# Places for the first rows of y, and the engine for the low parts of the output weights, in a hybrid gMLP and SSD layer on one core

## The chip, the cores and the metric

The kernel runs on one core of a Trainium2 chip. The metric is the device time of one execution in microseconds (us): the median of several runs. The profile comes from one more execution, whose own time is given beside its span.

Engines are named as in the profile: PE (TensorE, matmuls), DVE (VectorE), ACT (ScalarE), POOL (GpSimd), SP (SyncE, which here issues nearly all loads). Each takes its instructions in one fixed order and waits at the head of it.

## The reference, cut

One layer over 1024 positions of width 1024: a gMLP branch (y_a), a Mamba-2 SSD branch (y_b, 2048 wide, 8 groups), a gated merge, an output projection and a last normalisation. All inputs are float32.

```python
proj = h @ w_in
y_a = spatial_gating(gelu(gm_u), gelu(gm_v), ...) * silu(gm_z)
y_b = ssd_scan(xh, dt, a, bm, cm) + xh * d_skip[:, None]
yz = (y_b.reshape(b, s, 2048) * silu(ssm_z)).reshape(b, s, 8, 256)
y_b = rms_norm(yz, ssm_norm_w.reshape(8, -1)).reshape(b, s, 2048)
merged = sigmoid(g_a) * (y_a @ w_proj_a) + sigmoid(g_b) * (y_b @ w_proj_b)
x = x + gate[:, None, :] * (merged @ w_out)
return rms_norm(x, final_norm_w)
```

## The kernel before, in words

Large products run in fp32r with three matmuls for one: each operand is split into a high part (ACT casts it to fp32r) and a low part (the difference, cast again), and high by high, high by low and low by high are summed in PSUM. Besides, y_b @ w_proj_b and merged @ w_out are computed block by block with seven products instead of eight (Strassen's scheme): p1 to p7 for the first, seven of PRODUCTS for the second.

The kernel's last 300 us run through three stages that matter here.

**SSD.** `step` takes the 8 groups and their chunks one after the other. `front` makes the product sp of the states, `back` the product yn of the state before, and `evacuate` takes yn out of PSUM: DVE multiplies (ym, L1262), POOL adds and multiplies by the gate (L1264, L1265); the result is stored to DRAM (yb_d). Sums of squares over a group follow on POOL (L1293; L1285 for the last two groups), then matmuls with ones (pq) and a short chain that gives the factor of the RMS norm, rs_d in DRAM. Between these, `proj_a` fills PE with the matmuls of y_a @ w_proj_a (pma); `wa_load` loads its raw weights into a ring of four places, war_r.

**p1 to p7** (from L1636 on). `loads(u)` issues, six units ahead, on SP: for a unit with fresh rows `y_load` (first rb, the factor of a group, for even n; then yn, 128 rows of y), then the weights. `operands(u)`, four units ahead, normalises these rows (`y_norm`, DVE, in place) and splits them into `{p}bh`, `{p}bl`. The places of 128x512 come from a list, room, in which places are put in the order in which they come free, and from which each load takes the first. Three rings are cut from room: rb_r (factors), bh_r and bl_r (high and low parts). The order on each engine is that of a scheduler that follows the program with priorities and its own estimates; so a place decides what a load waits for, and can also move instructions.

**The output product.** `gate_load` and `merged` make the left operands: `split` gives a11, s1, s2, a22, s4, a12 their high and low parts, with s4 from `fourth` (L1786). `wo_load` loads a block of w_out, `wo_split` (L1795) makes its high part on ACT and its low part in place on DVE (L1798). A name such as wlt13 is the block t1 of quarter 3, `wlb110` the block b11 of quarter 0, wlt21 the block t2 of quarter 1. The places of high parts are reused under the name of the first that had them (ma11h, mwhb).

Of the kernel before, what the change touches and what calls it, by code (L numbers as in the profile page):

```python
# [35 lines left out]
def hybrid_kernel(  # L36
# [7 lines left out]
    V, A, G, PE = nc.vector, nc.scalar, nc.gpsimd, nc.tensor  # L44
# [42 lines left out]
    def f32(t):  # L87
        return t.bitcast(F32)
# [1284 lines left out]
    room = [f"{nm}{v}{k}" for nm in BN for v in "hl" for k in range(4)]  # L1373
# [4 lines left out]
    def ring(n):  # L1378

        return [room.pop(0) for _ in range(n)], [0]  # L1380
# [20 lines left out]
    war_r, wah_r, wal_r = [], [], []  # L1401
# [130 lines left out]
    tha_r, ea_r, y1_r, ym_r = (ring(c) for c in (4, 3, 2, 2))  # L1532
# [86 lines left out]
    def slot_tile(name, dt=F32):  # L1619
        tag = room.pop(0)  # L1620
        t = hp.tile([P, 512], dt, name=name, tag=tag)
        tags_of[name] = tag
        return t
# [12 lines left out]

    first, rest = room[:3], room[10:21]
    del room[10:21], room[:3]
    rb_r, bh_r, bl_r = (([first[n]] + [rest.pop(0) for _ in range(c)], [0]) for n, c in enumerate((3, 4, 4)))
    yt, rbs = {}, {}  # L1640

    def y_load(n, h):
# [89 lines left out]
    def place(name):  # L1732
        if not places and m_sl:
            pool, b = m_sl.pop(0)
            t = pool.tile([P, 3, 512], F32R, name=f"m{name}", tag="sl", bufs=b)
            places.extend(t[:, i] for i in range(3))
        return (places.pop(0), None) if places else (slot_tile(name, F32R), name)
# [57 lines left out]
    def wo_split(nm, j):  # L1795
        hi, t = place(f"wh{nm}{j}"), wor.pop((nm, j))
        A.copy(hi[0], f32(t))
        V.tensor_sub(t, f32(t), f32(hi[0]))  # L1798
        opb[nm, j] = [hi, (t, f"wl{nm}{j}")]

    rows = {}
# [21 lines left out]
            groups[7].post2(1, groups[7].late[:1])  # L1823
    draw(left[0] + 1)
    room.extend(tag for k in (KT - 2, KT - 1) for tag in ya_tags[k])
    for tags, _ in (war_r[0], wah_r[0], wal_r[0], tha_r):
        room.extend(tags)
    ps1.__exit__(None, None, None)
    ps3 = tc.tile_pool(name="ps3", bufs=1, space=PSUM, reuse_waits="tile")
# [3 lines left out]

    BESIDE = [(j // 2, wo_load, ("b11", j)) for j in range(4)] + [(2 + j, wo_load, ("t1", j)) for j in range(4)]
    BESIDE += [(2 + j, wo_split, ("b11", j)) for j in range(4)]
    BESIDE += [(3 + j, row_load, (j,)) for j in range(5)] + [(j + 4, split, ("s1", j - 1)) for j in (1, 3)]
    for u, (nm, k) in enumerate(units):
        if k == 0:
            if nm == "p1":
                first = {t: psb.tile([P, 512], F32, name=f"{t}p", tag=f"b{t}") for t in ('x0', 'x1', 'x2', 'x3', 'y3', 'y1', 'y2', 'y0')}  # L1840
# [25 lines left out]
        if k == KT - 1:  # L1866
            for j in range(4):
                with tc.high_priority():
                    if nm in ("p1", "p3", "p5"):
                        t = slot_tile(f"{nm}_{j}")  # L1870
# [83 lines left out]
    for nm, bn, pn, first, t0, c, done in PRODUCTS:  # L1954
# [4 lines left out]
        def beside(j):  # L1959
            if nm == "s1":  # L1960
                fourth(j)
            for b in LOADS.get(nm, ()):
                wo_load(b, j)
            if nm == "a11" and j < 3:
                row_load(5 + j)
            if (na, j) in raw:
                last["split"] = split(na, j).ins
            for b in SPLITS.get(nm, ()):
                wo_split(b, j)
# [34 lines left out]
    lo, hi = slice(0, 256), slice(256, 512)  # L2004
# [63 lines left out]
```

## Time and profile before

| | |
|---|---|
| median of 3 runs | 1365.38 us (1363.75 to 1366.4) |
| profiled execution | 1363.33 us, span 1361.5 us, granted PE clock 0.997 |
| PE busy | 99% of the span |
| DVE, ACT, POOL busy | 78%, 59%, 14% |
| L1264, L1265 (POOL, 128x512) | 1281 ns and 1386 ns in the mean |
| L1798 (DVE, 128x512) | 671 to 687 ns |
| L1652, normalisation of y (DVE) | 763 ns in the mean, 32 of them |

In the stages named above, by the clock of the span: SSD ends with the last pq matmuls at about 1122 us, p1 begins at 1123.59, the output product follows p4, whose last matmuls run about 1276, and the last stores end the span.

A row of a timeline reads: start in us, duration in us, engine, line, operation, output <- inputs with their shapes, and in brackets how long the engine stood idle before it and what released it.

### The profile page before, as it was taken

What the parts mean: (1) busy time and instruction counts of PE and PEld (TensorE: products, weight loads), DVE (VectorE), ACT (ScalarE), POOL (GpSimd) and SP (SyncE); (2) the same over time, 40 slices, a digit from 0 to 9 for tenths busy, and PEclk for the clock granted to TensorE, in tenths of its full rate; (3) what the DMA queues carried; (4) which work ended last, traced back from release to release, by engine and by line L of the source; (5) the groups of instructions that cost most, each with busy time, mean ns of one, the idle gap of its engine ahead of it and who ended that gap; (6) DMA issues with size and microseconds to landing.
All of it is one profiled execution on the core that took longest, in us unless ns stands there. A gap on an engine that the chain in (4) does not pass through costs nothing.

```text
span 1361.5 us, 20111 instructions
## 1 busy us (share of the span) xinstructions
PE 1347.4 (99%) x6907; PEld 1114.0 (82%) x6907; DVE 1055.5 (78%) x1731; ACT 801.4 (59%) x1446; POOL 195.4 (14%) x193
## 2 busy tenths in 40 slices
PE   8999999999999999999999999999999999999997
PEld 6688888888888888888888888888888888788886
DVE  5777786787777898687887788458888866959976
ACT  5754666666656665456576655486877743333443
POOL 1000000000000000000000000007898971000002
PEclk9999999999999999999999999999999999999999
DMA  9675444433345667777656865489889858978913
GB/s 294 174 249 151 123 124 124 118 123 117 108 125 155 193 190 228 243 233 237 199 194 189 248 203 184 159 289 312 306 293 313 306 207 313 332 260 314 381 45 124
DMA packets 249577, 288.64 MB, mean 212 GB/s; under 512 B 16860, under 2 KB 196484, under 8 KB 249476
## 3 DMA queue, kind: packets, MB, share of 16 engines
q1 hardware_dynamic: 174868, 203.80, 47.0%
q10 hardware_dynamic: 74544, 83.57, 18.0%
q8 instruction: 54, 0.88, 0.3%
q14 instruction: 47, 0.39, 0.1%
q0 software_dynamic: 64, 0.00, 0.0%
HBM read 199.82 MB, written 87.49 MB: 211 GB/s over the span
## 4 chain that ended last, share of the span: by engine, by line
PE 86%; DMA 8%; DVE 3%; SPq 1%; issue 1%; ACT 0%; POOL 0%; POOLq 0%; DVEq 0%; ACTq 0%
PE xcb L585 6%; PE xz L585 6%; PE xuz L585 6%; PE xx L585 6%; PE pma L82 6%; PE xg L585 6%; PE yuz L585 3%; PE yx L585 3%; PE ycb L585 3%; PE yz L585 3%; PE vx L990 3%; PE yg L585 3%; PE ox L1909 3%; PE yi L82 2%; PE sp L82 2%; PE oy L1909 2%
## 5 line engine op out<-in xcount | busy, mean ns | idle before, releaser
L1159 POOL TENSOR_SCALAR_AFFINE_SELECT dcy<-dcy 128x1024 f32<-128x1024 f32 x32 | 35.3, 1102 | 789.1 <-DMA yl<-ya_d 745.8
L1167 ACT ACTIVATE dcy<-dcy,nacs 128x128 f32<-128x128 f32 x256 | 78.3, 389 | 2.8 <-POOL dcy L1159 2.3
L1183 DVE TENSOR_TENSOR dcy<-dcy,pc 128x1024 f32<-128x1024 f32 x32 | 39.0, 1219 | 7.8 <-PE pc L85 5.7
L1265 POOL TENSOR_TENSOR yz<-y,sl 128x512 f32<-128x512 f32 x32 | 44.4, 1386 | 2.5
L82 PE MATMUL pma<-yh,wah 128*128 128x512 f32 x128 | 43.2, 418 | 0.0
L82 PE MATMUL pma<-yh,wal 128*128 128x512 f32 x128 | 42.6, 413 | 0.0
L82 PE MATMUL pma<-yl,wah 128*128 128x512 f32 x128 | 40.2, 395 | 0.0
L1155 ACT ACTIVATE ea<-dcy 64x512 f32<-64x512 f32 x64 | 39.8, 622 | 0.4
L1190 ACT COPY bn<-pc 128x256 f32<-128x256 f32 x32 | 11.9, 371 | 46.8 <-DVE dcy L1183 45.9
L1652 DVE SCALAR_TENSOR_TENSOR yn<-yn,par,rb 128x512 f32<-128x512 f32 x32 | 24.4, 763 | 17.9 <-DMA yn<-yb_d 16.2
L1060 ACT ACTIVATE ac<-ac 128x1024 f32<-128x1024 f32 x32 | 33.9, 1061 | 7.4 <-DVE ac L1058 7.3
L1058 DVE SCALAR_TENSOR_TENSOR ac<-c2x,cwt,ac 128x1023 f32<-128x1023 f32 (+2 forms) x24 | 30.7, 1280 | 8.7 <-ACT ac L1056 8.6
L1264 POOL TENSOR_TENSOR y<-y,ym 128x512 f32<-128x512 f32 (+1 forms) x32 | 37.0, 1155 | 2.1 <-DVE ym L1262 2.1
L1058 DVE SCALAR_TENSOR_TENSOR ac<-c2cb,cwt,ac 128x1023 f32<-128x1023 f32 (+2 forms) x24 | 30.7, 1279 | 8.1 <-ACT ac L1056 8.0
L1924 POOL TENSOR_TENSOR r<-r,fnw 128x512 f32<-128x512 f32 x4 | 6.1, 1533 | 205.3 <-ACT junk L1922 205.3
L82 PE MATMUL yi<-dcy,xd 128*64 128x128 f32 x512 | 35.0, 279 | 0.0
L1262 DVE TENSOR_TENSOR ym<-yn,ea 128x512 f32<-128x512 f32 (+1 forms) x32 | 19.9, 621 | 18.2 <-PE yn L82 18.1
L82 PE MATMUL sp<-xe,bn 128*128 128x256 f32 x112 | 32.7, 409 | 0.0
L82 PEld LDWEIGHTS yn<-sl,st 128*128 128x128 f32 x224 | 29.7, 191 | 2.8 <-POOL st L1228 0.4
L82 PEld LDWEIGHTS yi<-dcy,xd 128*64 128x64 f32 x512 | 27.3, 136 | 5.7 <-issue 2.9
L1058 DVE SCALAR_TENSOR_TENSOR ac<-c1cb,cwt,ac 128x1023 f32<-128x1023 f32 (+2 forms) x24 | 30.6, 1276 | 1.3 <-ACT ac L1056 1.3
L1022 ACT ACTIVATE vm<-vm,vr 128x128 f32<-128x128 f32 x64 | 25.6, 483 | 9.6 <-DMA vm<-v_d 9.1
(2983 smaller groups left out, 4369.7 us busy)
## 6 DMA issues: line engine op xcount, KB each, us to landing
sl<-s_d SPq DMA_DIRECT2D x32, 768.0 KB, 6.9
s_d<-ac ACTq DMA_DIRECT2D x32, 512.0 KB, 3.3
wb_d<-wbb ACTq DMA_DIRECT2D x32, 512.0 KB, 3.8
dcy<-acs_d SPq DMA_DIRECT2D x32, 512.0 KB, 4.6
av<-in_w_in_dram SPq DMA_DIRECT2D x36, 256.0 KB, 3.5
aw<-in_ada_w_dram SPq DMA_DIRECT2D x16, 512.0 KB, 6.1
wbr<-in_w_proj_b_dram SPq DMA_DIRECT2D x32, 256.0 KB, 4.5
yb_d<-yz ACTq DMA_DIRECT2D x32, 256.0 KB, 6.0
```

The costliest lines, as they stand in the source:

```text
L82: pin(PE.matmul(acc, l, r, start=first, stop=last))
L585: pin(PE.matmul(ps, lw[:, k * P : (k + 1) * P], r[k], start=first and n + k == 0, stop=n == 2 and k == 3, skip_group_check=not first))
L990: pin(PE.matmul(ps[pn][j], l[:, j * P : (j + 1) * P], r, start=nm in ("p1", "p5", "p2") and n + units[i][1] == 0, stop=n == 2 and k == 3, ...
L1058: V.scalar_tensor_tensor(ac[:, s:], cc[:, : S - s], conv_wt[:, 3 - s, i : i + 1], ac[:, s:], op0=ALU.mult, op1=ALU.add)
L1060: A.activation(ac, ac, AF.Silu)
L1155: link("A", lambda: A.activation(ea[hh * HD : (hh + 1) * HD], dcy.rearrange("p (j e) i l -> p e j (i l)", e=2)[hh * HD : (hh + 1) * HD, hh ...
L1159: link("G", lambda: G.affine_select(out=d8, in_=d8, compare_op=ALU.is_ge, fill=-1e30, base=0, pattern=[[0, 2 * HPG], [1, P]], channel_mult ...
L1167: link("A", lambda: A.activation(dcy[:, h, i, :], dcy[:, h, i, :], AF.Exp, bias=sub[:, i, h : h + 1]))
L1183: link("V", lambda: V.tensor_tensor(d3, d3, pc[:, 0:256].unsqueeze(1).to_broadcast([P, HPG, 256]), op=ALU.mult))
L1264: link("G", lambda: G.tensor_add(y1[:, :, t0:], y1[:, :, t0:], m[:, :, t0:]))
L1265: link("G", lambda: G.tensor_mul(yz, y1, sl[:, 4:6]))
L1909: pin(PE.matmul(ps, a[:, tsl], b[:, cs], start=first and n + j == 0, stop=n == 2 and j == 3, skip_group_check=not first))
```

## The change

Two things are changed.

The rings of p1 to p7 are cut anew. Before, each of rb_r, bh_r and bl_r got one of the three places first (which have held ea, the decays of the SSD stage) and the others from rest; now rb_r gets all three and one of rest, bh_r and bl_r five of rest each. And the four places of `wa_load` (war_r) are put at the front of room at once, instead of at its end after the last product of the first projection; so the first four loads of y (yn0 to yn3) take them. Before, yn0 took the place of the SSD state (st) and yn1 to yn3 places of y_a.

The low parts in `wo_split` are made by POOL instead of DVE: 28 operations of 128x512.

```diff
     first, rest = room[:3], room[10:21]
     del room[10:21], room[:3]
-    rb_r, bh_r, bl_r = (([first[n]] + [rest.pop(0) for _ in range(c)], [0]) for n, c in enumerate((3, 4, 4)))
+    rb_r, bh_r, bl_r = ((first[:n] + [rest.pop(0) for _ in range(c)], [0]) for n, c in ((3, 1), (0, 5), (0, 5)))
+    room[:0] = war_r[0][0]
...
     def wo_split(nm, j):
         hi, t = place(f"wh{nm}{j}"), wor.pop((nm, j))
         A.copy(hi[0], f32(t))
-        V.tensor_sub(t, f32(t), f32(hi[0]))
+        G.tensor_sub(t, f32(t), f32(hi[0]))
         opb[nm, j] = [hi, (t, f"wl{nm}{j}")]
...
     room.extend(tag for k in (KT - 2, KT - 1) for tag in ya_tags[k])
-    for tags, _ in (war_r[0], wah_r[0], wal_r[0], tha_r):
+    for tags, _ in (wah_r[0], wal_r[0], tha_r):
         room.extend(tags)
```

Lines behind L1639 count one more after the change.

SP keeps its order; only what its loads wait for changes. These are its rows at the first loads of y (behind each in brackets the engines whose counters it waits for; rb0 and yn0, yn1 are as in the text above, p1r the raw weights of p1):

```order
-L91 DMA yn0_0_10925<-yb_d0_91 128x512 [waits DMAHW3_49,DVE_49,PE_49]
-L91 DMA p1r0_10928<-in_w_proj_b_dram 128x512 [waits DMAHW5_49]
-L91 DMA yn1_0_10930<-yb_d1_92 128x512 [waits DMAHW0_49,PE_49]
-L91 DMA p1r1_10933<-in_w_proj_b_dram 128x512 [waits DMAHW2_49,Activation_49]
-L91 DMA rb2_0_10935<-rs_d1_59 128x512 [waits DMAHW4_49,PE_49]
-L91 DMA yn2_0_10937<-yb_d2_93 128x512 [waits DMAHW6_49]
+L91 DMA yn0_0_10925<-yb_d0_91 128x512 [waits DMAHW0_49]
+L91 DMA p1r0_10928<-in_w_proj_b_dram 128x512 [waits DMAHW2_49,DVE_49,PE_49]
+L91 DMA yn1_0_10930<-yb_d1_92 128x512 [waits DMAHW3_49]
+L91 DMA p1r1_10933<-in_w_proj_b_dram 128x512 [waits DMAHW4_49,DVE_49,Activation_49]
+L91 DMA rb2_0_10935<-rs_d1_59 128x512 [waits DMAHW5_49]
+L91 DMA yn2_0_10937<-yb_d2_93 128x512 [waits DMAHW7_49]
```

yn0 no longer waits for PE or DVE; p1r0, which now stands first in line with a wait for engines, waits for PE's product sp7_2 and p1r1 for DVE's ym6_3. (Before, yn0 waited for PE's last product yn7_3, and all that follows behind it.)

On DVE the normalisations of y have moved up. This is the end of the SSD stage after the change, from the evacuation of group 7's chunk pair 2 on; before, the rows of L1653 (then L1652) stood behind those of L1305:

```order
 L1236 TENSOR_TENSOR st22_8261<-st22_8261,sp7_2_10712 128x256
+L1653 SCALAR_TENSOR_TENSOR yn0_0_10925<-yn0_0_10925,par2_147,rb0_0_10923 128x512
 L1262 TENSOR_TENSOR ym7_2_10749<-yn7_2_10743,ea7_2_10375 128x512
 L1183 TENSOR_TENSOR dcy7_3_10526<-dcy7_3_10526,pc7_3_10754 128x1024
```

```order
+L1653 SCALAR_TENSOR_TENSOR yn1_0_10930<-yn1_0_10930,par2_147,rb0_0_10923 128x512
 L1262 TENSOR_TENSOR ym6_3_10804<-yn6_3_10799,ea6_3_10456 128x512
 L1236 TENSOR_TENSOR st_8258<-st_8258,sp7_3_10819 128x256
 L1216 SCALAR_TENSOR_TENSOR y17_3_10822<-sl7_3_10528,dskt_151,yi7_3_10810 128x256 x2
+L1653 SCALAR_TENSOR_TENSOR yn2_0_10937<-yn2_0_10937,par2_147,rb2_0_10935 128x512
 L1262 TENSOR_TENSOR ym7_3_10841<-yn7_3_10836,ea7_3_10530 128x512
```

Each of yn0, yn1 and yn2 is now normalised ahead of one of the last three evacuations, which wait for it in order.

On ACT, in the output product, the high part of a12 for quarter 2 has moved ahead of two high parts of weights. Before:

```order
L1797 CAST ma11h1_12273<-wlt12_12316 128x512
L1755 CAST ma11h1_12273<-s1_3_12190 128x512
L1797 CAST wht22_12558<-wlt22_12463 128x512
L1797 CAST mwhb112_12318<-wlt13_12345 128x512
L1755 CAST mwhb112_12318<-p1_0_11222 128x512
L1755 CAST a12h2_12904<-tg6_0_12341 128x512
```

After:

```order
L1798 CAST ma11h1_12273<-wlt12_12316 128x512
L1756 CAST ma11h1_12273<-s1_3_12190 128x512
L1756 CAST a12h2_12904<-tg6_0_12341 128x512
L1798 CAST wht22_12558<-wlt22_12463 128x512
L1798 CAST mwhb112_12318<-wlt13_12345 128x512
L1756 CAST mwhb112_12318<-p1_0_11222 128x512
```

a12h2 waits for DVE's s4_2 (`s4_2_12550`, L1786, now L1787). In the same stretch POOL, which had nothing to do there, now makes these low parts in this order:

```order
+L1799 TENSOR_TENSOR wlb110_12214<-wlb110_12214,ma11h0_12220 128x512
+L1799 TENSOR_TENSOR wlb111_12216<-wlb111_12216,ma11h1_12273 128x512
+L1799 TENSOR_TENSOR wlb112_12247<-wlb112_12247,mwhb112_12318 128x512
+L1799 TENSOR_TENSOR wlb113_12249<-wlb113_12249,mwhb113_12347 128x512
+L1799 TENSOR_TENSOR wlt10_12267<-wlt10_12267,ma11h0_12220 128x512
+L1799 TENSOR_TENSOR wlt21_12443<-wlt21_12443,wht21_12534 128x512
+L1799 TENSOR_TENSOR wlt11_12298<-wlt11_12298,ma11h1_12273 128x512
+L1799 TENSOR_TENSOR wlt12_12316<-wlt12_12316,ma11h1_12273 128x512
+L1799 TENSOR_TENSOR wlt22_12463<-wlt22_12463,wht22_12558 128x512
+L1799 TENSOR_TENSOR wlt13_12345<-wlt13_12345,mwhb112_12318 128x512
```

wlt13's low part is the tenth; 18 more follow. On DVE the same 28 rows are gone, and three operations stand ahead of p4bl7 that stood behind it.

## The prediction

> **What bounds the kernel now.** I read the page's shares first, then the chain that ended last, then busy time by stage, then what TensorE (PE) waits for.
>
> ```profile
> PE 1347.4 (99%) x6907; PEld 1114.0 (82%) x6907; DVE 1055.5 (78%) x1731; ACT 801.4 (59%) x1446; POOL 195.4 (14%) x193
> PE 86%; DMA 8%; DVE 3%; SPq 1%; issue 1%; ACT 0%; POOL 0%; POOLq 0%; DVEq 0%; ACTq 0%
> ```
>
> TensorE is busy 99% of the span and fills 86% of the chain. Work that other engines shed therefore gains only where TensorE is shown idle. The same view by stage (columns: stretch, length, busy time of PE, PEld, DVE, ACT, POOL) shows what stands close behind it:
>
> ```profile
> 1100.00:1150.00 50.00, 50.00 (x280) 40.46 (x279) 33.39 (x54) 17.30 (x32) 21.00 (x17) 1.00 0.71 244
> 1150.00:1200.00 50.00, 49.40 (x216) 39.97 (x215) 41.49 (x67) 13.85 (x24) 0.00 (x0) 1.00 0.92 331
> 1250.00:1300.00 50.00, 49.40 (x219) 40.56 (x217) 50.00 (x84) 22.56 (x40) 0.00 (x0) 1.00 0.97 366
> ```
>
> From 1250 to 1300 us VectorE (DVE) has no idle time, and there the new GpSimd work falls. TensorE's waits that the change can touch are two, each with its row in the timeline:
>
> ```profile
> PE oy L1909 <- DVE wlt L1798: 0.6, 1, 0.6
> PE x0p L1717 <- DVE p6bl L1691: 0.5, 1, 0.5
> 1290.02 0.39 PE L1909 MATMUL oy<-ma11h,s1l 128*128 128x512 f32 x1
> 1290.24 0.39 PE L1909 MATMUL oy<-mwhb,ma11h 128*128 128x512 f32 x1
> 1291.23 0.50 PE L1909 MATMUL oy<-wlt,ma11h 128*128 128x512 f32 x1 [0.60 <-DVE wlt L1798]
> 1167.13 0.39 PE L1717 MATMUL x0p<-p6bh,p6a 128*128 128x512 f32 x1
> 1168.06 0.50 PE L1717 MATMUL x0p<-p6bl,p6a 128*128 128x512 f32 x1 [0.55 <-DVE p6bl L1691]
> ```
>
> Matmuls otherwise start 0.22 to 0.23 us apart (1290.02 to 1290.24), so the first place loses about 0.9 us with its slow restart and the second 0.7, some 1.3 with smaller ones behind it. **All that the change can win is 2.2 us**, 0.16% of 1363.
>
> **Part A, the first rows of y.** Four loads of y go to places that are free; their places before were held until the last state product.
>
> ```profile
> 1095.90 0.37 SPq L91 DMA_DIRECT2D rb<-rs_d  x1
> 1110.42 0.32 SPq L91 DMA_DIRECT2D yn<-yb_d  x1
> 1112.82 0.32 SPq L91 DMA_DIRECT2D yn<-yb_d  x1
> ...
> DMA to landing us min/median/max: 4.4/5.5/6.5
> ```
>
> The first load now goes right behind rb, at about 1096.3 instead of 1110.42, and lands 4.4 to 6.5 us later (the last row gives all 24 loads of y): 1100.7 to 1102.8. SP runs in order, so p1r0 and p1r1, which inherit the waits, still hold what stands behind them; the second y goes when the product sp7_2 is done, the third after the evacuation ym6_3. Nothing in p1 (from 1123.59 on) waited for y, so early arrival is worth nothing there.
>
> But the normalisations of these rows have moved up in VectorE's order, and VectorE too runs in order: yn0's stands ahead of the evacuation ym7_2. Behind that evacuation hangs GpSimd's (POOL's) last chain:
>
> ```profile
> 1100.08 0.69 DVE L1262 TENSOR_TENSOR ym<-yn,ea 128x512 f32<-128x512 f32 x1 [1.55 <-PE yn L82]
> 1100.85 1.28 POOL L1264 TENSOR_TENSOR y<-y,ym 128x512 f32<-128x512 f32 x1 [0.60 <-DVE ym L1262]
> 1109.49 1.27 POOL L1293 TENSOR_TENSOR yz<-yz 128x512 f32<-128x512 f32 x1
> 1111.24 0.65 PE L82 MATMUL pq<-yz,ones 128*32 128x128 f32 x16
> 1118.13 1.46 POOL L1285 TENSOR_TENSOR lq<-lq,lq 128x512 f32<-128x512 f32 x1 [3.02 <-ACT lq L1281]
> 1121.73 0.43 PE L82 MATMUL pq<-lq,ones 128*32 128x128 f32 x8
> ```
>
> Step by step: yn0 lands at 1100.7, its normalisation takes 0.75 (row of 1117.69 below), so ym7_2 starts at about 1101.5, 1.4 late. From 1100.85 POOL works almost without a gap until 1110.76, the end of the sum of squares that the second half of these 16 pq matmuls reads. That half starts at about 1111.5, so the chain has 0.75 of slack. A second normalisation (yn1) falls beside the chain and holds one of its operations for 0.67, the cadence of such an operation. 1.4 + 0.67 − 0.75 = **+1.3 us** in which TensorE, in order, stands at pq. Bounds: 0, if yn0 lands before 1100.1 (some other transfer of this trace would have to be its model, none of the 24 is), 2.4 if it lands at the median and 3.4 at the slowest; I keep 0 to 3.4. The third normalisation delays ym7_3, but pq7_1, which hangs on it, comes only at 1121.73, 2.1 us after its sum ends (1118.13 + 1.46), and hides it.
>
> **Part B, p6.** Its stall hangs on rows that SP loads late:
>
> ```profile
> SPq L91 <- DMA rs_d<-ssq: 3.7, 1, 3.7
> ```
>
> That wait is for the factor of the last groups, not for a place. The re-cut rings leave it as it is: 0, with −1.3 as the other end.
>
> **Part C, the low parts on GpSimd.** Twenty-eight operations leave VectorE and enter POOL. On VectorE one starts 0.60 us after another. On POOL the same shape takes 1.27 to 1.29 where VectorE leaves it alone. What decides is whether the two run beside each other:
>
> ```profile
> 1113.82 1.29 POOL L1285 TENSOR_TENSOR lq<-lq,lq 128x512 f32<-128x512 f32 x1
> 1114.37 1.28 DVE L1652 SCALAR_TENSOR_TENSOR yn<-yn,par,rb 128x512 f32<-128x512 f32 x1 [1.66 <-issue]
> 1117.69 0.75 DVE L1652 SCALAR_TENSOR_TENSOR yn<-yn,par,rb 128x512 f32<-128x512 f32 x1 [2.03 <-DMA yn<-yb_d]
> 1340.52 3.51 DVE L1932 SCALAR_TENSOR_TENSOR r<-r,dde,fnw 128x1024 f32<-128x1024 f32 x2
> 1341.49 1.45 POOL L1924 TENSOR_TENSOR r<-r,fnw 128x512 f32<-128x512 f32 x1 [3.03 <-ACT junk L1922]
> 1345.15 1.27 DVE L1932 SCALAR_TENSOR_TENSOR r<-r,dde,fnw 128x1024 f32<-128x1024 f32 x1
> 1345.52 2.06 POOL L1924 TENSOR_TENSOR r<-r,fnw 128x512 f32<-128x512 f32 x1 [2.58 <-ACT junk L1922]
> 1102.16 0.68 DVE L1186 TENSOR_TENSOR xd<-px,dthq 128x512 f32<-128x512 f32 x1
> 1102.21 1.29 POOL L1265 TENSOR_TENSOR yz<-y,sl 128x512 f32<-128x512 f32 x1
> ```
>
> They do not. A normalisation beside POOL's sum takes 1.28, alone 0.75; two L1932 beside one POOL operation take 3.51, where the single one of 1345.15 takes 1.27, so one POOL operation's length is added. POOL's operation of 2.06 us waited in turn for that single one. With two operands in SBUF on both sides they take turns, one and one, even with VectorE's next operation queued. The last pair shows the exception: a VectorE operation that reads PSUM (px) runs beside POOL undisturbed.
>
> [...]
>
> So VectorE is not relieved: each low part that falls beside it costs it POOL's 1.25 instead of its own 0.60. The path to the matmul of 1291.23:
>
> ```profile
> 1285.09 0.67 DVE L1786 TENSOR_TENSOR s<-tg,p 128x512 f32<-128x512 f32 x1
> 1285.76 0.62 ACT L1797 CAST mwhb<-wlt 128x512 fp32r<-128x512 f32 x1
> 1286.80 0.62 ACT L1755 CAST a12h<-tg 128x512 fp32r<-128x512 f32 x1
> 1290.51 0.67 DVE L1798 TENSOR_TENSOR wlt<-wlt,mwhb 128x512 fp32r<-128x512 f32 x1
> ```
>
> Before, ACT made wlt13's high part at 1285.76, ahead of a12h2, and VectorE its low part at 1290.51. Now a12h2 stands ahead of the high parts of wlt22 and wlt13 in ACT's order, and it waits for VectorE's s4_2, the row of 1285.09.
> - Ahead of s4_2, eight low parts run on POOL (wlb110 to wlb113, wlt10, wlt21, wlt11, wlt12) while VectorE is full: 8 × 1.25, less 0.6 that falls beside an operation that reads PSUM: +9.4. Five low parts have left VectorE there: −3.0. One other operation now stands behind s4_2: −0.6. So s4_2 ends at 1285.7 + 5.8 = 1291.5.
> - Then ACT's a12h2, wht22 and wlt13's high part at 0.52 each: 1293.1.
> - POOL first makes wlt22's low part, from about 1292.5 with a turn of VectorE before it, to 1294.2, lets one VectorE operation through (0.6), and ends wlt13's low part at 1296.1. TensorE reads it at 1291.23 now: **+4.9 us**.
>
> Some 1.5 to 2 us of this appear already at the last step of p4:
>
> ```profile
> 1271.26 0.67 DVE L1691 TENSOR_TENSOR p4bl<-yn,p4bh 128x512 fp32r<-128x512 f32 x1
> 1274.83 0.39 PE L1717 MATMUL x0p<-p4bl,p4a 128*128 128x512 f32 x1
> ```
>
> VectorE's p4bl7 is ready 2.9 before its matmul; four low parts at 0.65 more and three operations put ahead of it at 0.60 make it 4.4 late. That is part of the 4.9, since a TensorE held here arrives later there. What comes after has this room:
>
> ```profile
> 1300.00:1362.00 62.00, 54.71 (x253) 45.62 (x251) 43.07 (x79) 26.12 (x61) 9.01 (x9) 0.97 0.17 68
> ```
>
> The remaining 18 low parts cost VectorE 0.65 each, but from 1300 on it has 19 us of idle time (43.07 busy of 62); I add 0.3. **C = +5.2.** Bounds: if VectorE were not held at all, POOL's six low parts from wlt10 to wlt13, begun at about 1282.7 at 1.27 each, end at 1290.3 and the stall goes: −0.9. If each low part took 2.06 (the longest POOL row of the shape) instead of 1.27, the eight on the path add 8 × 0.8 = 6.4: +11.6.
>
> **The sum.** A +1.3, B 0, C +5.2: +6.5 us. The profiled execution took 1363.33 us (span 1361.5), so 1369.8; the median of the three runs, 1365.38, lies 2.05 above the profiled one, so the median becomes 1371.9, say **1372.0**.
>
> **Rivals.**
> 1. *VectorE is truly relieved* (the other side): POOL's writes rounded to fp32r, in place, do not take turns with VectorE, or the turns fall into gaps. Then C is −0.9, and with y early p6 may gain up to 1.3; part A hidden. Time 1365.4 − 0.9 to − 2.2: 1363.2 to 1364.5, within 0.2%. It decides by one point: whether s4_2 ends before about 1286. For it: nothing between 1250 and 1300 uses POOL today (0.00), so no row shows this mixture. Against it: every pair of such operands above, without exception, took turns.
> 2. *The low part is dear on POOL*: 2.06 us each, or POOL is served only after several VectorE operations, since none of the rows has a VectorE queue that is full for 50 us. C up to +11.6: 1378.3. Against it: the undisturbed rows are all at 1.27 to 1.29, and the row of 3.51 shows POOL served at once.
> 3. *Part A does nothing*: y lands in time or the pq slack is larger; only C counts. 1370.6. For it: the slack is read from one group of 16 matmuls whose halves the row doesn't part. Against: none of 24 loads landed under 4.4 us.
> 4. *The weights' part is not on the path*: a12h2 does not hold ACT, because s4_2 is early enough. Then wlt13's low part is the last of six in POOL from 1283.3 on, each of 1.27 with a turn of 0.6 after it: about 1294.5 against 1291.23: C +3.3, A +1.3, 1370.0.
>
> **How the numbers follow.** The sum 0.58 (with its own spread of 1368 to 1376), rival 1 0.13, rival 2 0.11, rival 3 0.10, rival 4 0.08. The range 1366.5 to 1378.5 leaves out rival 1 and the upper part of rival 2. A measurement of this kernel can tell about 0.2%, 2.7 us, from no change. Faster by more would need more than the 2.2 us that TensorE idles at these places: 0.03. Within 0.2%: rival 1 and the low edge of the other cases: 0.17. Slower: 0.80.
>
> **What would show it.** A: an idle time of about 1.3 us ahead of the pq matmuls near 1111, with ym7_2's row starting after yn0's normalisation near 1101.5. No such gap: A is wrong. C: VectorE rows of 1.8 to 1.9 us between 1262 and 1300 beside POOL rows of L1799, s4_2 ending near 1292 to 1294, TensorE idle by about 2 us at the end of p4 and about 3 more at `oy<-wlt`, now released by POOL. VectorE rows that stay at 0.67 beside POOL rows would refute the turns and with them the forecast. B: the 0.55 at p6 stays.

## The result and the profile after

The changed kernel takes 1369.96 us in the median of 22 runs (1364.68 to 1373.29), the one before 1366.43 us in the same runs: **ratio 1.003, interval 1.002 to 1.0039**, 3.5 us slower by the medians. In a second set of runs (experiment e1) it was 1.0026 (1.0015 to 1.0038). The profiled execution took 1364.68 us, span 1363.0, granted clock 0.999; it is the shortest of the 22.

The page's first lines and TensorE's waits (us in all, times, longest) answer to those of before:

```profile
PE 1346.4 (99%) x6907; PEld 1113.5 (82%) x6907; DVE 1054.6 (77%) x1703; ACT 800.4 (59%) x1446; POOL 251.9 (18%) x221
PE oy L1910 <- POOL wlt L1799: 2.0, 1, 2.0
PE pq L82 <- POOL yz L1293: 0.9, 1, 0.9
PE yn L82 <- DVE st L1236: 0.3, 1, 0.3
```

Twenty-eight operations have left VectorE, yet its busy time has fallen by only 0.9 us, while POOL's has risen by 56.5, 1.6 times what 28 operations of 1.28 need. Most of what left VectorE as work (28 rows of about 0.67, 18.8 us) came back to it as waiting within its rows. TensorE's waits have changed places: p6's is gone, pq has a new one, and that for the low part wlt13 has grown from 0.6 to 2.0 us and comes from POOL now.

Part A in the timeline of VectorE, POOL and TensorE:

```profile
1100.88 0.75 DVE L1653 SCALAR_TENSOR_TENSOR yn<-yn,par,rb 128x512 f32<-128x512 f32 x1 [2.76 <-DMA yn<-yb_d]
1101.55 0.68 DVE L1262 TENSOR_TENSOR ym<-yn,ea 128x512 f32<-128x512 f32 x1
1105.59 1.73 DVE L1653 SCALAR_TENSOR_TENSOR yn<-yn,par,rb 128x512 f32<-128x512 f32 x1
...
1102.32 1.30 POOL L1264 TENSOR_TENSOR y<-y,ym 128x512 f32<-128x512 f32 x1 [2.47 <-DVE ym L1262]
1111.40 1.26 POOL L1293 TENSOR_TENSOR yz<-yz 128x512 f32<-128x512 f32 x1
...
1112.71 0.43 PE L82 MATMUL pq<-yz,ones 128*32 128x128 f32 x8 [0.92 <-POOL yz L1293]
```

VectorE stands at yn0 for 2.76 us with the evacuation ym7_2 behind it, and POOL's chain ends 1.9 us later than before although the execution was 0.4 earlier until then. Part C, first on POOL, then on VectorE, ACT and TensorE:

```profile
1260.31 15.34 POOL L1799 TENSOR_TENSOR wlb<-wlb,ma11h 128x512 fp32r<-128x512 f32 x2 [124.21 <-DMA wlb<-wo_d]
1275.60 3.00 POOL L1799 TENSOR_TENSOR wlb<-wlb,mwhb 128x512 fp32r<-128x512 f32 x2
1280.62 1.50 POOL L1799 TENSOR_TENSOR wlt<-wlt,ma11h 128x512 fp32r<-128x512 f32 x1 [2.02 <-DVE s L1787]
1290.68 1.72 POOL L1799 TENSOR_TENSOR wlt<-wlt,mwhb 128x512 fp32r<-128x512 f32 x1
...
1270.90 1.88 DVE L1783 TENSOR_TENSOR p<-p,p 128x512 f32<-128x512 f32 x3
1272.88 1.61 DVE L1757 TENSOR_TENSOR s2l<-p,s2h 128x512 fp32r<-128x512 f32 x1
1280.27 0.68 DVE L1757 TENSOR_TENSOR a22l<-p,a22h 128x512 fp32r<-128x512 f32 x1
1280.88 1.78 DVE L1770 TENSOR_TENSOR tg<-tg,ma 128x512 f32<-128x512 f32 x1
1282.58 1.78 DVE L1787 TENSOR_TENSOR s<-tg,p 128x512 f32<-128x512 f32 x1
1284.28 1.77 DVE L1770 TENSOR_TENSOR tg<-tg,ma 128x512 f32<-128x512 f32 x1
1285.98 1.78 DVE L1787 TENSOR_TENSOR s<-tg,p 128x512 f32<-128x512 f32 x1
...
1287.85 0.62 ACT L1756 CAST a12h<-tg 128x512 fp32r<-128x512 f32 x1 [3.60 <-DVE s L1787]
1292.45 0.50 PE L1910 MATMUL oy<-wlt,ma11h 128*128 128x512 f32 x1 [2.02 <-POOL wlt L1799]
```

Two different things are seen. From 1280 on the two engines take turns: many VectorE operations take 1.78 instead of 0.67. But the first two low parts together took 15.34 us, and no single VectorE operation between 1260 and 1272.8 is any longer than 0.68: there POOL waited and VectorE did not; the first of the two rows alone is 13.64 long. At 1272.8, where s2l had to wait a moment (0.1) for ACT, POOL got in.

Between the two profiles (starts of the first matmuls of a stage): TensorE is 0.40 earlier at 1098.6, 1.21 later where p1 begins, 0.19 earlier where p4 begins, 0.20 earlier where the output product begins and 1.20 later at the last matmul. So A cost 1.6 us, p1 to p7 gave back 1.4 (at p6), the end of p4 cost nothing, and the output product cost 1.4. The median says more than this one execution, 3.5 us and not 1.2; the experiments ask where that is.

### The profile page after: what moved, and what is told of

Read it like the earlier page. It is cut to its first block, busy times and chain, and to the rows that moved or that the text cites. A ratio compares the mean times of both kernels' runs of the same rounds, so it can differ in the third digit from the quotient of the medians.

```text
span 1363.0 us, 20108 instructions
## 1 busy us (share of the span) xinstructions
PE 1346.4 (99%) x6907; PEld 1113.5 (82%) x6907; DVE 1054.6 (77%) x1703; ACT 800.4 (59%) x1446; POOL 251.9 (18%) x221
## 5 line engine op out<-in xcount | busy, mean ns | idle before, releaser
L1799 POOL TENSOR_TENSOR wlb<-wlb,ma11h 128x512 fp32r<-128x512 f32 x5 | 19.7, 3942 | 124.2 <-DMA wlb<-wo_d 124.2
L1653 DVE SCALAR_TENSOR_TENSOR yn<-yn,par,rb 128x512 f32<-128x512 f32 x32 | 25.9, 813 | 17.5 <-DMA yn<-yb_d 17.5
L1058 DVE SCALAR_TENSOR_TENSOR ac<-c2x,cwt,ac 128x1023 f32<-128x1023 f32 (+2 forms) x24 | 30.7, 1280 | 8.5 <-ACT ac L1056 8.4
```

The costliest lines, as they stand in the source:

```text
L1058: V.scalar_tensor_tensor(ac[:, s:], cc[:, : S - s], conv_wt[:, 3 - s, i : i + 1], ac[:, s:], op0=ALU.mult, op1=ALU.add)
L1653: V.scalar_tensor_tensor(t, t, snw[:, n : n + 1], rbs[n // 2, h], op0=ALU.mult, op1=ALU.mult)
```

## The experiments

**e1, the change once more.** No edit.

> The changed kernel once more, to see whether its profile of 1364.7 us (three stalls of TensorE: 0.92 at pq, 2.02 at oy<-wlt, none at p6) is the usual one, since the median of its 22 runs, 1369.96, lies 5.3 above that. Theory 1 (same stalls in every execution, the rest is the granted clock): the same three stalls within 0.3 us, and the span differs from 1363.0 by about 2 us for each 0.001 of clock below 0.999. Theory 2 (GpSimd's turns fall differently from execution to execution): the stall at oy<-wlt differs by more than 1 us from 2.02 or others appear.

Span 1364.1, stalls 0.92 at pq, 0.34 at yn, 2.40 at `oy<-wlt`; ratio 1.0026 (1.0015 to 1.0038). The same three stalls, the last 0.38 longer: a little more than theory 1 allowed, and far from theory 2's 1 us.

**e2, the places alone.**

```diff
-        G.tensor_sub(t, f32(t), f32(hi[0]))
+        V.tensor_sub(t, f32(t), f32(hi[0]))
```

> Only the places of y are changed, the low parts stay on VectorE. Theory 1: TensorE stalls at pq near 1112 as with the whole change (0.9 to 1.2, 1.6 us of matmul starts in all), p6's stall of 0.55 is gone (1.4 in all), oy<-wlt waits 0.6 as before: ratio 1.000 (0.999 to 1.001). Rival (the places cause the whole +3.5 us, by the clock or otherwise): ratio 1.002 or more.

Ratio **1.000** (0.9991 to 1.0009). The stalls at pq (0.92) and yn (0.26) are there, none at p6, and none at `oy<-wlt` either. The places cost and give back about the same.

**e3, GpSimd alone** (the kernel before with the low parts on POOL).

```diff
-        V.tensor_sub(t, f32(t), f32(hi[0]))
+        G.tensor_sub(t, f32(t), f32(hi[0]))
```

> Only the low parts move to GpSimd. Theory 1: no stall at pq, p6 stalls 0.55 as before, oy<-wlt waits about 2.0 instead of 0.6: +1.4 us in the profile, ratio 1.001. Rival (the turns cost most of the +3.5 us in the usual run): ratio 1.002 to 1.003. My sum on record had +5.2 us for this part, ratio 1.004.

Ratio **1.004** (1.0027 to 1.0052), 5.5 us. Theory 1's 1.4 falls; the sum on record had 5.2. TensorE has two stalls, and something behind them. First its timeline, then two stretches (columns as in the prediction's views by stage; the 1.00 and 0.83 ahead of the last two are the granted clock):

```profile
1293.02 0.50 PE L1909 MATMUL oy<-wlt,ma11h 128*128 128x512 f32 x1 [1.39 <-POOL wlt L1798]
1295.24 0.50 PE L1909 MATMUL oy<-mwhb 128*128 128x512 f32 x1 [1.72 <-DVE mwhb L1756]
1295.58 0.40 PE L1909 MATMUL oy<-ma11h,mwhb 128*128 128x512 f32 x1
1295.82 0.40 PE L1909 MATMUL oy<-wlt,mwhb 128*128 128x512 f32 x1
...
1298.45 0.63 PE L1909 MATMUL oy<-ma11h,s1l 128*128 128x512 f32 x1
1298.87 0.63 PE L1909 MATMUL oy<-mwhb,ma11h 128*128 128x512 f32 x1
```

```profile
1280.00:1290.00 10.00, 10.00 (x46) 8.19 (x44) 10.00 (x9) 5.32 (x10) 7.19 (x6) 1.00 1.03 395
1290.00:1300.00 10.00, 6.89 (x22) 4.81 (x21) 10.00 (x11) 4.76 (x9) 10.00 (x7) 0.83 0.81 296
```

The second stall is not for a low part of POOL at all: it is for s1's low part, which VectorE makes and which POOL's turns have delayed. And shortly after it the matmuls start 0.43 apart instead of 0.24, and the granted clock is 0.66 from 1295 to 1300. 0.83 over 10 us is 1.7 us lost on top of the stalls.

**e4, the places with the normalisations behind ym7_3** (low parts on VectorE).

```diff
-        V.scalar_tensor_tensor(t, t, snw[:, n : n + 1], rbs[n // 2, h], op0=ALU.mult, op1=ALU.mult)
+        with tc.issue_after(last["V"]):
+            V.scalar_tensor_tensor(t, t, snw[:, n : n + 1], rbs[n // 2, h], op0=ALU.mult, op1=ALU.mult)
```

> The places of y are changed, but the normalisations of y stay behind the last evacuation ym7_3 in VectorE's order, and the low parts stay on VectorE. Theory 1: no stall at pq (0 instead of 0.92), and p6's stall stays away because the rows of y come early: -1.4 us, ratio 0.999. Rival (p6 stalls less only because TensorE itself is 1.2 us later and its rows are not): p6's stall of 0.55 comes back, ratio 1.000.

A miss: ratio 1.0011 (1.0002 to 1.002). The stall at the first pq is gone, as theory 1 has it, but TensorE stands 1.78 us at the last one, and the clock is 0.83 from 1120 to 1130.

```profile
1125.13 0.42 PE L82 MATMUL pq<-lq,ones 128*32 128x128 f32 x8 [1.78 <-POOL lq L1285]
1122.58 1.15 ACT L1281 ACTIVATE lq<-yz 128x512 f32<-128x512 f32 x2 [9.43 <-DMA yb_d<-yz]
```

The normalisations took POOL's turns in its last chain (its operations there take 1.62 to 1.74), and the products tha6, which now stand behind them, hold up ACT's stores, behind which the squares of the last sum wait until 1122.58. A new wait took the place of the old.

**e5, the kernel before once more.** No edit.

> The kernel before once more, for a second profile of it: e3 shows no stall at p6 although its places are those of before. Theory 1 (p6's stall belongs to the places): 0.55 at p6 again. Rival (it differs from execution to execution, by when the loads land): it is absent or differs by more than 0.3.

The rival: no stall at p6, none at `oy<-wlt`, but one in p1, where the profile on which the prediction rests had none:

```profile
1143.32 0.50 PE L1717 MATMUL x0p<-p1bl,p1a 128*128 128x512 f32 x1 [1.42 <-DVE p1bl L1691]
...
DMA to landing us min/median/max: 4.4/6.1/7.3
```

The slowest load of y landed in 7.3 us instead of 6.5 in the first profile, and p1 ran out of rows. With the old places the three profiles show 0.55 at p6, 1.42 in p1, and nothing (e3); with the new ones none of seven shows a stall in p1 or p6.

**e6, a12h2 back behind wlt13's high part**, three rows later on ACT; no other row moves.

```diff
-        A.copy(hi[0], f32(t))
+        cast[nm, j] = A.copy(hi[0], f32(t))
...
-        A.copy(hi[0], t)
+        with ExitStack() as behind:
+            if nm == "a12":
+                behind.enter_context(tc.issue_after(cast["t1", 3].ins))
+            A.copy(hi[0], t)
```

> The whole change, but on ACT the high part of a12h2 stands behind that of wlt13, three rows later; nothing else moves. Theory 1 (the stall comes over a12h2, which waits for s4_2 ahead of the weights' high parts): ACT makes wlt13's high part about 3.5 us earlier, GpSimd its low part 2.5 to 3.5 earlier, the stall at oy<-wlt falls from 2.0 to 2.4 down to 0 to 0.6, ratio 1.000 to 1.0012. Rival (the turns of GpSimd and VectorE alone make the low parts late): stall 1.4 or more, ratio 1.0025.

Ratio 1.0033 (1.0021 to 1.0044): not better. ACT makes wlt13's high part earlier, and TensorE no longer waits for wlt13, but for what VectorE still makes:

```profile
1292.40 0.73 PE L1913 MATMUL oy<-ma11h,ma11h 128*128 128x512 f32 x2 [0.82 <-DVE ma11h L1760]
1297.45 0.75 PE L1913 MATMUL oy<-mwhb 128*128 128x512 f32 x1 [3.39 <-DVE mwhb L1760]
...
1292.27 1.78 DVE L1790 TENSOR_TENSOR s<-tg,p 128x512 f32<-128x512 f32 x1
1293.97 1.75 DVE L1760 TENSOR_TENSOR a22l<-p,a22h 128x512 fp32r<-128x512 f32 x1
1295.64 1.75 DVE L1760 TENSOR_TENSOR mwhb<-s,ma11h 128x512 fp32r<-128x512 f32 x1
```

VectorE does one operation in 1.70 us here. ACT's order decides only which of the late operands TensorE meets first; the turns make them late.

**e7, the blocks t1 and t2 back on VectorE**, the other 20 low parts on POOL.

```diff
-        G.tensor_sub(t, f32(t), f32(hi[0]))
+        (V if nm in ("t1", "t2") else G).tensor_sub(t, f32(t), f32(hi[0]))
```

> The whole change, but the low parts of the blocks t1 and t2 (8 of 28) stay on VectorE; the other 20 are made by GpSimd. Theory 1 (only low parts on the path to oy<-wlt cost time): stall there 0 to 0.6, no drop of the granted clock near 1295, ratio 1.000 to 1.001. Rival (any low part of GpSimd beside the full VectorE costs): a stall of 1 us or more between 1275 and 1330, ratio 1.002.

Ratio 1.0011 (1.0001 to 1.0021); the stall at `oy<-wlt` is 0.24, the clock does not drop. POOL's wlb110 to wlb113 still run between 1261.8 and 1280, and TensorE has no stall there. Eight low parts of 28, those in the stretch just ahead of the matmuls that read them, carry most of the cost of part C; the interval leaves the other 20, with the places, up to 2.9 us.

**e8, the turns by themselves.** A kernel with only streams of VectorE additions and four GpSimd subtractions in each (`prev` is the addition before, `q` is in PSUM):

```diff
+            if kind == "chain":
+                pin(V.tensor_add(d[i], prev, src[i % 2]))
+            elif kind == "psum" and i % 4 == 3:
+                pin(V.tensor_add(d[i], q, src[i % 2]))
+            else:
+                pin(V.tensor_add(d[i], src[i % 2], src[2 + i % 2]))
```

> Not the layer: only four streams of 30 VectorE additions of 128x512, in each of which GpSimd starts four subtractions of that size when the 7th addition is done (the output is a copy of input rows). Streams: free (independent, two operands in SBUF), chain (each reads the one before), psum (every fourth reads PSUM), rounded (as free, GpSimd's results fp32r). Theory 1 (taking turns, as on record): in every stream GpSimd's first subtraction takes at most 2.1 us and the VectorE additions beside it 1.7 to 1.9. Theory 2 (VectorE keeps GpSimd out as long as its own stream of such operations has no gap, as the first low part's 13.6 to 14.2 us suggest): in free and chain the first subtraction lasts until the stream ends, about 14 us, in psum until the next addition that reads PSUM, up to 2.5 us. Theory 3 (the first fp32r operation on GpSimd is slow by itself): only rounded shows a long first one.

POOL's rows by stream (fr free, ch chain, qq psum, rr rounded), and VectorE's beside the first two:

```profile
11.96 14.89 POOL L75 TENSOR_TENSOR frg<-frtrig,src 128x512 f32<-128x512 f32 x1 [11.52 <-DVE frtrig L72]
36.13 1.77 POOL L75 TENSOR_TENSOR chg<-chtrig,src 128x512 f32<-128x512 f32 x1 [5.63 <-DVE chtrig L67]
37.86 5.04 POOL L75 TENSOR_TENSOR chg<-src,src 128x512 f32<-128x512 f32 x3
61.27 1.26 POOL L75 TENSOR_TENSOR qqg<-qqtrig,src 128x512 f32<-128x512 f32 x1 [18.37 <-DVE qqtrig L72]
62.49 5.05 POOL L75 TENSOR_TENSOR qqg<-src,src 128x512 f32<-128x512 f32 x3
83.06 14.89 POOL L75 TENSOR_TENSOR rrg<-rrtrig,src 128x512 fp32r<-128x512 f32 x1 [15.52 <-DVE rrtrig L72]
...
11.79 13.93 DVE L72 TENSOR_TENSOR frd<-src,src 128x512 f32<-128x512 f32 x23
36.81 19.71 DVE L67 TENSOR_TENSOR chd<-chd,src 128x512 f32<-128x512 f32 x22
```

In the stream of independent additions POOL's first row lasts 14.89 us, to 1.1 us after the end of the stream: it waited for the whole stream, and the 23 additions ran at 0.60 each, undisturbed. Where each addition reads the one before, POOL came in at once, and both took turns (1.70 for each of POOL's, 1.63 for an addition instead of 0.69). In the third stream it came in at an addition that reads PSUM, and from then on its next operations, queued behind, took turns although the additions are independent (5.05 for its next three, 4.70 for the three additions behind that one). With fp32r the first row is 14.89 too. Theory 2 holds for free and rounded, and for POOL's first operation in psum; theory 1 for chain; theory 3 falls.

This does not cover all of the layer. At 1280.62 (part C above) POOL had been idle, and it came in at once, between two VectorE operations 0.61 apart; the second, `tg<-tg,ma`, neither reads the one before it nor PSUM. What opened the way there is not shown.

**e9, the places with the normalisations in VectorE's gaps** (yn0 behind y16_3, yn1 behind y17_3, the rest behind tha6; low parts on VectorE; `fronts` and `last["tha", dd]` hold those instructions).

```diff
+        with tc.issue_after(fronts[-2 + n] if (n, h) in ((0, 0), (1, 0)) else last.get(("tha", KT - 2), last["V"])):
             V.scalar_tensor_tensor(t, t, snw[:, n : n + 1], rbs[n // 2, h], op0=ALU.mult, op1=ALU.mult)
```

> The places of y changed, low parts on VectorE, and the normalisations put where VectorE idles in the SSD stage: yn0 behind the row y16_3, yn1 behind y17_3, the others behind tha6 (L1526). ACT's order is that of e2 but for one store. Theory 1 (the stall at pq comes from ym7_2 standing behind yn0): no stall at pq nor at yn (0.9 and 0.3 in e2), and yn early keeps p1 and p6 free of stalls: about 1.4 us less than e2, ratio 0.998 to 1.000. Rival (GpSimd's chain is held by the normalisations wherever they stand): a stall at pq of 0.5 or more, ratio as e2 or above.

Ratio 0.9993 (0.9984 to 1.0002), 1362.65 against 1363.47 us. No stall at the first pq, at yn, in p1, p6 or at `oy<-wlt`; 0.80 at the last pq, behind late squares on ACT as in e4. Its interval is clear of that of the changed kernel, but its gain over the kernel before, 0.8 us, is not clear of none.

**e10, the clock after stalls.** Sixty streams of matmuls with waits of five lengths between them.

> Not the layer: 60 streams of 36 to 50 matmuls of 128x512 (8 to 11 us each), between them a wait for one to five VectorE operations in a row, 12 of each (the output is a copy of input rows). Theory 1 (a stall of TensorE costs its own length only): the matmuls behind every wait start 0.23 us apart again after at most 0.4 us. Theory 2 (a stall of about 1.7 us or more can halve the granted clock for some 3.4 us, by chance): behind waits under 1.2 us no slow matmuls, behind those of 1.7 to 2.5 us in some of 12 matmuls 0.43 us apart for about 3.4 us, behind those over 3.4 us in all.

Five streams in a row (in brackets the wait before each; a matmul at full clock takes 0.227):

```profile
346.00 8.95 PE L69 MATMUL acc<-op,w 128*128 128x512 f32 x38 [0.79 <-DVE op L75]
356.46 10.49 PE L69 MATMUL acc<-op,w 128*128 128x512 f32 x45 [1.51 <-DVE op L75]
369.20 8.68 PE L69 MATMUL acc<-op,w 128*128 128x512 f32 x37 [2.24 <-DVE op L75]
380.84 11.88 PE L69 MATMUL acc<-op,w 128*128 128x512 f32 x44 [2.96 <-DVE op L75]
396.41 10.95 PE L69 MATMUL acc<-op,w 128*128 128x512 f32 x36 [3.69 <-DVE op L75]
```

The first three run at 38, 45 and 37 × 0.227 plus 0.3; the fourth is 1.6 longer than that, the fifth 2.5. Over the whole run slow matmuls (0.43 apart) followed none of 12 waits of 0.79 us, none of 12 of 1.51, one of 12 of 2.24, 11 of 12 of 2.96 and all 11 of 3.69, and in the streams from 304 us on each of them cost 1.4 to 2.8 us. Theory 2, with a higher bound than it gave.

By its length alone a stall of 2.24 seems to draw the clock by chance (one of 12), and e4's 1.78 to contradict e10 (none of 12 at 1.51, one at 2.24). The records of the granted clock in the traces tell more. Between the ends of each of these eleven traces they change only on a grid of 3.41 us (in the profile before: half from 16.55 to 19.96, then full for 392 times as long, to 1357.99). Count TensorE's idle time by the pieces of this grid, in e10 (198 pieces at full clock) and in the ten profiles of the layer (some 395 in each): each piece at full clock with 1.78 us or more idle was followed by one at half clock, and none with 1.71 or less was.

| run | stall, us | idle in one piece, us | the piece behind it |
|---|---|---|---|
| e4 | 1.78 | 1.78 | half |
| e3 | 1.39 and 1.72 | 1.91 | half |
| e6 | 3.39 | 3.34 | half |
| the change | 2.02 | 1.38 | full |
| e1 | 2.40 | 1.71 | full |

Counted by pieces these rows agree, and by length they do not: e4's stall fell into one piece, and those of the change and of e1 were cut by the edge of one. A halved piece, 3.41 us at half clock, costs 1.7 us by that count.

## Why the prediction held, and where it did not

Forecast 1372.0 (1366.5 to 1378.5), slower at 0.80; measured 1369.96, ratio 1.003. Forecast as a difference it was +6.5 us, and measured +3.5, so the direction held and the size was about twice too large; the kernel before came out 1 us higher in the 22 runs than in the three of them that the sum started from. A's mechanism held, C's in one half; B was mis-sized, and one step of C was wrong.

The terms can be read by stage, from the starts of TensorE's matmuls in every profile (us):

| run | A: from the matmuls that make yn for ym7_2 to p1 | B: p1 to the output product | C: output product, first matmul to last |
|---|---|---|---|
| before, e5 | 24.60, 24.59 | 153.73, 154.61 | 77.11, 76.19 |
| e3 (low parts on POOL) | 24.60 | 152.83 | 81.69 |
| e2 (places) | 26.40 | 152.32 | 76.19 |
| after, e1 (both) | 26.21, 26.29 | 152.32, 152.32 | 78.51, 79.12 |
| e6 | 26.54 | 152.32 | 82.63 |
| e7 | 26.79 | 152.32 | 76.89 |
| e9 | 25.55 | 152.34 | 76.20 |

e4 is left out, since a halved clock lies across its A and B.

- **A, +1.3.** Right. yn0's normalisation ended where the sum put it, ym7_2 started at 1101.55 (1101.5 forecast), and pq stalled 0.92 with 0.26 more at yn. By the table it costs 1.6 to 2.2 us.
- **"Nothing in p1 … waited for y, so early arrival is worth nothing there", and B, 0.** Wrong, and the reason why A does not show in the time. That was read from one execution. e5 has 1.42 in p1; with the new places p1 and p6 are free of stalls in seven profiles. By the table the new places gain 0.5 to 2.3 us here, 1.4 in the mean of the three profiles with the old ones, and e2 measures A and B together: 1.000.
- **C, +5.2.** The size is right for e3, the low parts alone: 5.5 us (3.7 to 7.1), the same by the table. In the whole change it is 3.5 beside e2's 1.000, and 2.3 and 2.9 in the two profiles (over the 76.19 of e2 and e5). Its working is right in one half. VectorE paid for POOL's operations in turns (1.78 instead of 0.67), and the path to wlt13 runs as written, over s4_2, a12h2 and two high parts to POOL's 1292.40. But it ended 3.7 us earlier than the 1296.1 forecast, because **the step "eight low parts run on POOL … while VectorE is full" failed**: the first waited for a pause, and the first four together lengthened VectorE's rows by only 1.6 us (1.61, 0.87 and 1.19 instead of 0.67). The other four cost VectorE 1.1 each, not 1.25. s4_2 ended at 1287.76, not 1291.5. The sentence "they take turns, one and one, even with VectorE's next operation queued" was drawn from single meetings of two operations, none in a long stream. In e8's gapless stream of independent operations POOL was kept out: its row of 14.89 begins at 11.96, and 22 of VectorE's additions began after it and ran ahead of it. In the layer p4bl7 was on time, and the 2 us at the end of p4 never came.
- **a12h2, which "stands ahead of the high parts of wlt22 and wlt13 in ACT's order"** and waits for s4_2, as what makes wlt13 late: true of the rows (ACT stands 3.60 for it), but not the cause of the cost. Undone in e6, the cost stays, at s1's low parts.
- **What no term held**: s1's low parts, made by VectorE, were late too (1.72 in e3, 3.39 in e6), and in e3 two stalls close together, 1.91 us idle in one piece, were followed by a halved clock, 1.7 us. Together they fill the room that the missing 3.7 us left, so that C came out at 5.2 is in part luck.
- **Rivals.** Rival 1 (VectorE relieved) falls by the rows of 1.78. Rival 2's second half, POOL served only after several operations, was real ahead of 1272.8, but made the change cheaper, not dearer. Rival 3 comes out in e2's time, for another reason than the one given: A costs what it was forecast to, and B gives it back. Rival 4's condition falls by ACT's wait of 3.60 for s4_2, though e6 bears out that the order on ACT does not decide the cost.

Of the 5.5 us by which e3's output product is longer than e5's, two stalls make 3.1 and the clock 1.7; the other 0.7, the slow restarts among it, is not parted.

## What to carry to other kernels

Twenty-eight subtractions with two operands in SBUF moved from a full VectorE to GpSimd lowered VectorE's busy time by 0.9 us here. Where the two engines took turns, VectorE paid 0.9 to 1.1 us of waiting (1.63 instead of 0.69 in e8, 1.78 instead of 0.67 in the layer) for an operation that it did in 0.60 itself; where GpSimd was kept out, it waited until VectorE paused (rows of 14.89 in e8, 13.6 to 14.2 in the layer). So before such a move look in a trace for what the two engines' rows do side by side. Move only what has time until then (20 of 28 low parts here), and count what VectorE still makes behind it. A load that arrives early is worth something only if its consumer does not stand, in order, ahead of work that is due sooner (yn0's stood ahead of ym7_2, and pq waited 0.92); and stalls of one profile should be seen in a second before they are added or left out.

## What the runs showed of the hardware

- In e8 GpSimd was kept out of a gapless stream of independent VectorE operations with two operands in SBUF: its row is 14.89 us long. In the layer the row of the first low part, in a stretch of VectorE without a gap, is 13.6 to 14.2 us long in five profiles. In e8 GpSimd took turns at once where each operation reads the one before (its first row is 1.77), and went on taking turns (5.05 for three) after it had come in at an operation that reads PSUM. In the layer it also came in at once where neither holds (1.50 at 1280.62); why is open.
- Between the ends of the eleven traces the granted clock changed only on a grid of 3.41 us, and it halved after every piece of it in which TensorE was idle for 1.78 us or more, after none with 1.71 or less. In e3 two short stalls in one piece (1.91 together) were followed by a drop, and stalls of 2.02 and 2.40 that lay across an edge (1.38 and 1.71 in one piece) were not.
- At the start of the span the clock was down for no piece (after, e7), one (before, e1, e6, e9) or two (e2 to e5): 0, 1.7 or 3.4 us' worth. The first drop agrees with the same count (1.50 us idle or less in a piece without one, 1.85 or more with one; 2.53 in the profile before). By it alone two profiles of one kernel differ by 1.7 us (before and e5, after and e1).
